# Output projections of a two-layer decoder trunk: all sums and low parts on VectorE, the first projection's sums made in layer A's heads, two plain tiles at the head of pass two

## The chip, the core and the metric

The kernel runs on one core of a Trainium2 chip. The metric is the device time of one execution in microseconds (us), as the median of several runs.

## The reference

One inference step of a trunk with two layers. The input is 1024 prompt tokens and 8 sample tokens, T = 1032 columns of 1024 features. Layer A is an HGRN2 mixer with 8 heads, layer B a chunked gMLP. Each ends in an output projection from 2048 to 1024 features, a residual add, and a gated per-layer embedding:

```python
# layer A
return (o * jax.nn.silu(z)) @ w_out, S          # z, o: (B, L, 2048), w_out: (2048, 1024)
# layer B
y = (u * s * jax.nn.silu(z)) @ w_out
# trunk, in each layer
h = h + y
gate = jax.nn.sigmoid(rmsnorm(h, norm_ple[i]) @ w_ple_gate[i])
h = h + gate * (p[i] @ w_ple_proj[i])
```

The change touches the two products with `w_out` and what lies just around them.

## The kernel before, in words

**Columns.** The 1032 tokens stand in the free dimension, in three column groups c = 0, 1, 2 of 384, 384 and 264. An output tile m (0 to 7) is 128 output features. The product's input, 2048 features deep, was stored to DRAM by the mixer as `ozd[c]`, 16 blocks of 128 features.

**Precision.** Every fp32 product is three products of rounded operands (`mm3`, lines 222 to 224): high x high, high x low, low x high. An operand's high part is a ScalarE (ACT) copy, its low part a subtraction (`split`, lines 217 and 218; in lists of loads lines 370 and 373; for weights 149 and 150). The low part's buffer is called `xml` or `bl`, the high part's `xmh` or `bh`.

**Units.** For columns c = 0 and 1 and two output tiles m, m+1 together, `unit` computes a 2 x 2 block product with seven block products instead of eight (twelve matmuls each): it needs sums of weight blocks (s1 to s4, made by GpSimd, the POOL engine, lines 191 to 198) and sums of data blocks (t1 to t4, made by `mix_rows`, lines 963 to 966). ACT copies the first product to `u2` (line 914). VectorE (DVE) adds further products to it at lines 918, 930, 937, 944 and 950. Line 937 gives `c` (the tile `c22`) from the bank `ps_d`. The unit's seventh product is added up in that same bank, so TensorE (PE) must wait for line 937 when it has done the sixth. Column group 2 is done plainly (24 matmuls of 264 columns a tile). A plain tile has 24 matmuls for each of the three groups.

**Projection.** `out_phase` runs twice: for layer A from about 760 to 960 us, for layer B from about 1624 to 1820. It goes over the depth in two passes f of 1024 features. Pass f=0: plain tiles 0 and 1, then units m = 2, 4, 6. Pass f=1: units m = 0, 2, 4, then plain tiles 6 and 7. Beside the plain tiles of pass one, `mix_first` makes the first half's sums and splits. During units m = 2 and 4, `mix_second` makes those of the second half and stores them to DRAM. During unit m = 6 the second half's blocks and sums replace the first half's: `jobs` loads them through seven buffers (three `zr`, four `raw`) in list order, each waiting for its high and low part. The low parts alternate between VectorE and GpSimd. `add` (line 1036) adds a result to the residual rows `h`: from PSUM on VectorE, from SBUF in pass one on GpSimd. In pass two `accum_sq` squares the new rows on ACT (line 257, into one of four `tmp` buffers), and GpSimd adds the squares up (line 258).

**Order.** TensorE's order is the order of the code. The other engines' streams, SP's queue of transfers among them, are put in order by a scheduler by readiness and priorities. Each stream then runs in that order. An instruction that waits holds up all behind it on its engine.

Of the kernel before, what the change touches and what calls it, by code (L numbers as in the profile page):

```python
# [17 lines left out]
P = 128  # L18
# [63 lines left out]
def trunk_kernel(ctx, tc, xT, st, pT, nrm, wina, lbl, gna, wouta, winb, lng, lnb, lngr, lnbr,  # L82
# [161 lines left out]
    def accum_sq(sp, ssq, src, first, last, w, eng=G):  # L244
# [3 lines left out]
        sq = sp.tile([P, 384], F32, name="sql", bufs=1) if last else sp.tile([P, 384], F32, name="tmp", bufs=4)  # L248
# [154 lines left out]
    def p_in_act(l, stage, load=True):  # L403
# [7 lines left out]
        return ([fh[:, :, OFF[c]:OFF[c] + W[c]] for c in CH], [fl[:, :, OFF[c]:OFF[c] + W[c]] for c in CH])  # L411

# [548 lines left out]
    def mix_rows(b11, b12, b21, b22, eng=V):  # L961

        V.tensor_tensor(b11, b12, b11, ALU.subtract)
        eng.tensor_tensor(b12, b22, b12, ALU.subtract)
        V.tensor_tensor(b22, b22, b11, ALU.subtract)
        V.tensor_tensor(b21, b21, b22, ALU.subtract)

    tdr = {}

    def out_phase(key, b, ssq, first, done, pre, begin):  # L970
# [3 lines left out]
        with ExitStack() as s:  # L974
# [14 lines left out]
            def quarters(k, rows):  # L989

                for (c, o), t in zip(((0, 0), (1, 0), (0, 4), (1, 4)), rows):
                    nc.sync.dma_start(t, ozd[c][:, k + o, :])


            rows = [[hr[c][2 * j + i] for i in range(2) for c in (0, 1)] for j in range(4)]
            if pre:
                rows[0] = [raw() for _ in range(4)]
            begin(up, raw, rows, quarters, load_h)

            def mix_first():  # L1000
                for j in range(4):
                    mix_rows(*rows[j], G)
                    for n, t in (("t2", rows[j][3]), ("t1", rows[j][0]), ("t3", rows[j][1])):
                        split(b[n][0][:, j, :], b[n][1][:, j, :], t, G if n == "t3" else V)
                    if not j and not pre:
# [37 lines left out]
            tk.spawn(mix_first(), 1)  # L1043
# [6 lines left out]
            for c in CH:  # L1050
                add(1, c, plain(pp.tile([P, 384], F32, name="ps_o1", tag=("pA", "po", "pt")[c], bufs=1), wt, c), False)
                if c == 1:
                    while any(p[2].__name__ == "mix_first" for p in tk.procs):
# [8 lines left out]
            if not tdr:  # L1062
                for n in ("t1", "t2", "t3", "t4"):
                    tdr[n] = dram.tile([P, 4, 384], F32, name="d" + n)

            def mix_second():
                for j in range(4):
# [5 lines left out]
                    for n, x in zip(("t1", "t3", "t4", "t2"), t):  # L1073
                        nc.sync.dma_start(tdr[n][:, j, :], x)
# [4 lines left out]
            def quarter(n, to=None):  # L1079
                src = {"b11": ozd[0][:, 8:12], "b21": ozd[0][:, 12:16], "b12": ozd[1][:, 8:12],  # L1080
                       "b22": ozd[1][:, 12:16]}.get(n)
                src = tdr[n] if src is None else src
                return [(src[:, k, :], b[to or n][0][:, k, :], b[to or n][1][:, k, :], 384) for k in range(4)]

            def jobs():
# [4 lines left out]
                turns = itertools.cycle([zr] * ZR + [lambda w: raw()[:, :w]] * 4)  # L1090
# [485 lines left out]
```

## Time and profile before

| | us |
|---|---|
| runs, median (lowest to highest, 3 runs) | 1933.72 (1931.68 to 1934.5) |
| profiled execution | 1930.22 |
| its span | 1928.5 |
| PE busy | 1870.2 |
| DVE busy | 1329.4 |
| ACT busy | 865.7 |
| POOL busy | 586.9 |

The profiled execution lies 3.5 us under the median. The mean granted TensorE clock was 0.986 of full speed. Busy time is shown for each engine. In a row of a timeline stand the start, the duration, engine, line, operation, output <- inputs, and in brackets the idle time before it with what ended it. A row of a window has its bounds, its length, the busy time and the count of instructions by engine, the granted clock, the share of the DMA engines and GB/s.

### The profile page before, as it was taken

The page shows a single profiled execution, that of the slowest core. Times are in us where ns is not written, and L with a number is a line of the kernel's source. Part 1 is how long each engine was busy: PE and PEld are TensorE (multiplying, and loading weights), DVE is VectorE, ACT ScalarE, POOL GpSimd, SP SyncE. Part 2 cuts the span into 40 slices and gives each one's busy share as a digit, 9 for nine tenths or more (in the row PEclk, how much of TensorE's full clock was granted, in tenths as well). Part 3 has the DMA queues.
Part 4 walks back from the last instruction along what each step waited for, and adds up shares of the span by engine and source line. Part 5 has one row for each costly group of instructions (what it writes and reads, how often), then busy time and mean ns, then how long its engine had stood idle before and what let it go on. Part 6 is the DMA issues. An engine that isn't in the chain of part 4 may idle for free.

```text
span 1928.5 us, 34355 instructions
## 1 busy us (share of the span) xinstructions
PE 1870.2 (97%) x13106; PEld 1840.3 (95%) x13106; DVE 1329.4 (69%) x2841; ACT 865.7 (45%) x1855; POOL 586.9 (30%) x563
## 2 busy tenths in 40 slices
PE   9999999999999999889999999999999999989997
PEld 8999999999999998889999999999999999889997
DVE  5967776776767676877564755577777777875655
ACT  6463544444454546344343544433434435343342
POOL 4110000001000100466432433345445442565421
PEclk8999999999999999999999999999999999999998
DMA  6232322222231326773233343323333237762223
GB/s 212 74 118 65 115 67 102 78 80 89 80 107 50 110 93 186 252 228 105 81 119 123 123 141 91 99 80 102 130 109 105 100 116 227 237 212 73 70 89 110
DMA packets 145109, 228.98 MB, mean 119 GB/s; under 512 B 13936, under 2 KB 120112, under 8 KB 143920
## 3 DMA queue, kind: packets, MB, share of 16 engines
q1 hardware_dynamic: 144944, 226.78, 36.1%
q8 instruction: 103, 1.69, 0.4%
q14 instruction: 62, 0.51, 0.1%
HBM read 167.62 MB, written 59.11 MB: 118 GB/s over the span
## 4 chain that ended last, share of the span: by engine, by line
PE 77%; DVE 8%; DMA 7%; issue 3%; POOL 2%; ACT 2%; SPq 1%; DVEq 0%; ACTq 0%; POOLq 0%
PE ps_proj L222 19%; PE ps_proj L224 19%; PE ps_proj L223 19%; PE ps_d L222 2%; PE ps_d L224 2%; PE ps_d L223 2%; DMA raw<-ozd 1%; PE psp L1376 1%; PE pC L679 1%; DVE wlo L150 1%; PE pt_o L725 1%; PE pss L272 1%; DMA dt<-raw 1%; PE p L645 1%; PE ps_o L222 1%
## 5 line engine op out<-in xcount | busy, mean ns | idle before, releaser
L222 PE MATMUL ps_proj<-bh,whi 128*128 128x384 f32 (+1 forms) x2448 | 784.7, 321 | 4.1 <-ACT pple_t L341 1.6
L224 PE MATMUL ps_proj<-bh,wlo 128*128 128x384 f32 (+1 forms) x2448 | 768.8, 314 | 3.1 <-DVE wlo L150 2.8
L223 PE MATMUL ps_proj<-bl,whi 128*128 128x384 f32 (+1 forms) x2448 | 767.4, 313 | 2.2 <-POOL bl L218 2.2
L222 PEld LDWEIGHTS ps_proj<-bh,whi 128*128 128x128 f32 x2448 | 464.2, 190 | 6.4 <-ACT pple_t L341 1.7
L223 PEld LDWEIGHTS ps_proj<-bl,whi 128*128 128x128 f32 x2448 | 464.4, 190 | 2.9 <-POOL bl L218 2.9
L224 PEld LDWEIGHTS ps_proj<-bh,wlo 128*128 128x128 f32 x2448 | 462.7, 189 | 4.5 <-DVE wlo L150 4.5
L150 DVE TENSOR_TENSOR wlo<-wstg,whi 128x1024 fp32r<-128x1024 f32 x148 | 193.7, 1308 | 107.1 <-ACT whi L149 106.0
L149 ACT CAST whi<-wstg 128x1024 fp32r<-128x1024 f32 x148 | 155.0, 1048 | 152.0 <-PE ps_proj L223 140.7
L149 ACT CAST shi<-ssum 128x512 fp32r<-128x512 f32 x136 | 84.0, 620 | 164.7 <-PE ps_proj L223 78.0
L150 DVE TENSOR_TENSOR slo<-ssum,shi 128x512 fp32r<-128x512 f32 x136 | 110.0, 810 | 23.3 <-ACT shi L149 23.0
L258 POOL TENSOR_TENSOR ssq<-ssq,tmp 128x384 f32<-128x384 f32 (+1 forms) x72 | 75.5, 1051 | 155.7 <-ACT tmp L257 146.8
L218 POOL TENSOR_TENSOR ql<-q,qh 128x384 fp32r<-128x384 f32 (+1 forms) x24 | 22.3, 928 | 254.5 <-ACT qh L217 254.5
L222 PE MATMUL ps_proj<-xmh,shi 128*128 128x384 f32 x248 | 84.3, 340 | 2.4 <-ACT xmh L217 2.1
L223 PE MATMUL ps_proj<-xml,shi 128*128 128x384 f32 x248 | 83.4, 336 | 2.3 <-DVE xml L218 2.3
L191 POOL TENSOR_TENSOR ssum<-wstg 128x512 f32<-128x512 f32 x34 | 50.3, 1480 | 111.4 <-DMA wstg<-in_winb 75.2
L231 POOL TENSOR_TENSOR rsq<-ss_e,mhalf 128x3 f32<-128x3 f32 (+2 forms) x32 | 24.1, 752 | 195.4 <-DVE ss_e L719 195.4
L224 PE MATMUL ps_proj<-xmh,slo 128*128 128x384 f32 x248 | 83.2, 336 | 0.0
L682 DVE TENSOR_TENSOR q<-q,t 128x192 f32<-128x192 f32 (+1 forms) x144 | 47.2, 329 | 44.5 <-PE pC L679 38.2
L257 ACT ACTIVATE tmp<-h 128x384 f32<-128x384 f32 (+1 forms) x72 | 35.3, 491 | 91.9 <-DVE h L1131 49.2
L193 POOL TENSOR_TENSOR ssum<-ssum,wstg 128x512 f32<-128x512 f32 x34 | 45.6, 1341 | 95.3 <-DVE slo L150 95.3
L1385 POOL TENSOR_TENSOR s<-s,u 128x384 f32<-128x384 f32 (+1 forms) x48 | 53.1, 1106 | 68.9 <-DVE s L1379 68.3
L1130 DVE TENSOR_TENSOR tmp<-tmp,pj 128x384 f32<-128x384 f32 (+1 forms) x48 | 25.0, 521 | 56.6 <-ACT tmp L1129 47.1
(330 smaller groups left out, 4062.2 us busy)
## 6 DMA issues: line engine op xcount, KB each, us to landing
wstg<-in_wina SPq DMA_DIRECT2D x48, 512.0 KB, 3.6
wstg<-in_winb SPq DMA_DIRECT2D x48, 512.0 KB, 4.4
raw<-ozd SPq DMA_DIRECT2D x44, 192.0 KB, 3.5
pj<-ppd SPq DMA_DIRECT2D x16, 516.0 KB, 4.8
S<-in_st SPq DMA_DIRECT2D x16, 512.0 KB, 5.3
vb<-vd SPq DMA_DIRECT2D x16, 512.0 KB, 4.6
out_so_s<-S SPq DMA_DIRECT2D x16, 512.0 KB, 3.4
wstg<-in_wouta SPq DMA_DIRECT2D x16, 512.0 KB, 4.5
```

What stands on the lines that cost most here:

```text
L149: A.copy(hi, src)
L150: V.tensor_tensor(lo, src, hi.bitcast(F32), ALU.subtract)
L191: G.tensor_tensor(t, a21, a22, ALU.add)
L193: G.tensor_tensor(t, t, a11, ALU.subtract)
L222: PE.matmul(ps, wh, xh, start=first, stop=False, skip_group_check=more)
L223: PE.matmul(ps, wh, xl, start=False, stop=False, skip_group_check=more)
L224: PE.matmul(ps, wl, xh, start=False, stop=last, skip_group_check=more)
L257: A.activation(sq[:, :w], src, AF.Square)
L258: eng.tensor_tensor(ssq, ssq, sq[:, :w], ALU.add)
L682: V.tensor_tensor(ql[:, :, 1, :], ql[:, :, 1, :], t2[:, :, 0:1].broadcast_to([P, n, lv]), ALU.mult)
L1130: V.tensor_tensor(gt[:, :w], gt[:, :w], pj[:, OFF[c]:OFF[c] + w], ALU.mult)
L1385: G.tensor_tensor(s[:, :w], s[:, :w], us[mm, c][:, :w], ALU.mult)
```

## The change

1. `mix_rows`, the low parts of the projections and the adds to `h` all run on VectorE. In each projection four subtractions and four low parts of the first sums, nine adds, and the low parts that alternated in the list of loads leave GpSimd. It keeps the weight sums and the sums of squares.
2. For the first projection, the sums of the first half are made by `mix_early` beside the heads of layer A: 16 loads, 16 subtractions and 16 stores of 192 KB. The projection then loads the sums in place of the blocks.
3. Pass two begins with plain tiles 0 and 1 in place of unit m = 0.
4. The second half's plain blocks are loaded ahead of its sums, into other buffers than before, and the loads go on between the plain tiles.
5. The squares of a projection's tiles go through one buffer, `sql`.

The core of the diff:

```diff
@@ out_order: the order of the weights, and so of the output tiles
-                [("O" + l, m, 1) for m in range(0, KT - 2, 2)] + [("o" + l, m, 1) for m in range(KT - 2, KT)])
+                [("o" + l, m, 1) for m in range(2)] + [("O" + l, m, 1) for m in range(2, KT - 2, 2)] +
+                [("o" + l, m, 1) for m in range(KT - 2, KT)])
@@ accum_sq
-    def accum_sq(sp, ssq, src, first, last, w, eng=G):
+    def accum_sq(sp, ssq, src, first, last, w, eng=G, own=False):
...
-        sq = sp.tile([P, 384], F32, name="sql", bufs=1) if last else sp.tile([P, 384], F32, name="tmp", bufs=4)
+        sq = sp.tile([P, 384], F32, name="sql", bufs=1) if last or own else sp.tile([P, 384], F32, name="tmp", bufs=4)
@@ mix_rows and quarters move up, out of out_phase
-    def mix_rows(b11, b12, b21, b22, eng=V):
+    def mix_rows(b11, b12, b21, b22):
...
-        eng.tensor_tensor(b12, b22, b12, ALU.subtract)
+        V.tensor_tensor(b12, b22, b12, ALU.subtract)
...
+    TS = ("t1", "t2", "t3", "t4")
+    tdr = [{n: dram.tile([P, 4, 384], F32, name=f"d{i}{n}") for n in TS} for i in range(3)]
+
+    def store_sums(d, j, rows):
+        for n, x in zip(("t1", "t3", "t4", "t2"), rows):
+            nc.sync.dma_start(d[n][:, j, :], x)
@@ in the heads of layer A
+    def mix_early():
+
+        for j in range(4):
+            t = [wa.tile([P, 2, 384], F32, name="zstg", bufs=2) for _ in range(2)]
+            t = [x[:, i, :] for x in t for i in range(2)]
+            quarters(j, t)
+            yield 8
+            mix_rows(*t)
+            store_sums(tdr[0], j, t)
+            yield 6
...
     for h in range(NH):
+        if h == 5:
+            tk.spawn(mix_early(), 4)
@@ out_phase: first sums
-            def mix_first():
+            def sums_first():
                 for j in range(4):
-                    mix_rows(*rows[j], G)
-                    for n, t in (("t2", rows[j][3]), ("t1", rows[j][0]), ("t3", rows[j][1])):
-                        split(b[n][0][:, j, :], b[n][1][:, j, :], t, G if n == "t3" else V)
+                    if not ahead:
+                        mix_rows(*rows[j])
+                    for n in ("t2", "t1", "t3"):
+                        split(b[n][0][:, j, :], b[n][1][:, j, :], rows[j][at[n]])
@@ out_phase: adds
-                eng = V if end or src.space == PSUM else G
                 with tc.high_priority(offset=PRI if end and m >= KT - 2 else 0):
-                    eng.tensor_tensor(hr[c][m], hr[c][m], src[:, :W[c]], ALU.add)
+                    V.tensor_tensor(hr[c][m], hr[c][m], src[:, :W[c]], ALU.add)
                 if end:
-                    accum_sq(sp, ssq[c], hr[c][m], c not in seen, m == KT - 1, W[c])
+                    accum_sq(sp, ssq[c], hr[c][m], c not in seen, m == KT - 1, W[c], own=True)
@@ out_phase: the exchange of halves, and pass two
-                todo = quarter("b11") + quarter("t2") + quarter("b21")
-                todo += [(ozd[2][:, 8 + k, :], b["c2"][0][:, k, :], b["c2"][1][:, k, :], W[2]) for k in range(8)]
-                todo += quarter("t1") + quarter("t3") + quarter("b22") + quarter("t4")
-                return load_list(todo, lambda w: next(turns)(w), ZR + 4, False, (V, G), True)
-                        then = {2: 4, 3: 4, 4: 4, 5: 8, 6: 4, 7: 4}
-                    elif (f, m) == (1, 0):
-                        then = {3: 4, 4: 4}
+                o = dict(b)
+                for n, to in (("b11", "b11"), ("b21", "t2"), ("b12", "b21"), ("b22", "t1"),
+                              ("t2", "t3"), ("t1", "b22"), ("t3", "t4"), ("t4", "b21")):
+                    b[n] = o[to]
+                todo = quarter("b11") + quarter("b21") + quarter("b12") + quarter("b22")
+                todo += [(ozd[2][:, 8 + k, :], b["c2"][0][:, k, :], b["c2"][1][:, k, :], W[2]) for k in range(8)]
+                todo += quarter("t2") + quarter("t1") + quarter("t3") + quarter("t4")
+                gen[0] = load_list(todo, lambda w: next(turns)(w), ZR + 4, False, (V,), True)
...
+            units(0, range(2, KT, 2), {2: (rows_of(2), {4: 1}), 4: (rows_of(4), {2: 1, 4: 1, 7: 1}),
+                                       KT - 2: (exchange, {2: 4, 3: 4, 4: 4, 6: 4, 7: 4})})
+            for m in range(2):
+                wt = take(key, m, 1)
+                for c in CH:
+                    ps = plain(bank(), wt, c)
+                    if (m, c) != (1, 2):
+                        steps(gen[0], 4)()
+                    add(m, c, ps, True)
+            units(1, range(2, KT - 2, 2), {KT - 4: (last_exchange, {4: 4})})
@@ begin of the first projection
-            quarters(j, rows[j])
+            for n, t in zip(("t1", "t3", "t4", "t2"), rows[j]):
+                nc.sync.dma_start(t, tdr[0][n][:, j, :])
```
How this moves instructions is shown at three places. The first is VectorE in unit m = 6 of the first projection, the last rows up to the `c` result, before:

```order
1555 L1036 TENSOR_TENSOR h_6_10170<-h_6_10170,ps_proj 128x384
1556 L150 TENSOR_TENSOR wlo<-wstg,whi 128x1024
1557 L373 TENSOR_TENSOR xml_10147<-zr,xmh_10146 128x384
1558 L373 TENSOR_TENSOR bl_123<-zr,bh_120 128x384
1559 L1036 TENSOR_TENSOR h_7_10187<-h_7_10187,ps_proj 128x264
1560 L373 TENSOR_TENSOR bl_123<-raw,bh_120 128x384
1561 L373 TENSOR_TENSOR bl_125<-raw,bh_122 128x264
1562 L930 TENSOR_TENSOR u_11063<-ps_proj,u_10963 128x384
1563 L150 TENSOR_TENSOR slo<-ssum,shi 128x512
1564 L373 TENSOR_TENSOR bl_125<-zr,bh_122 128x264
1565 L373 TENSOR_TENSOR bl_125<-raw,bh_122 128x264
1566 L937 TENSOR_TENSOR c_11094<-ps_d,u_11063 128x384
```
and after:

```order
1568 L374 TENSOR_TENSOR xml_10215<-raw,xmh_10214 128x384
1569 L1057 TENSOR_TENSOR h_6_10238<-h_6_10238,ps_proj 128x384
1570 L151 TENSOR_TENSOR wlo<-wstg,whi 128x1024
1571 L374 TENSOR_TENSOR xml_10215<-raw,xmh_10214 128x384 x2
1572 L374 TENSOR_TENSOR xml_10215<-zr,xmh_10214 128x384
1573 L1057 TENSOR_TENSOR h_7_10255<-h_7_10255,ps_proj 128x264
1574 L374 TENSOR_TENSOR bl_135<-zr,bh_132 128x384 x2
1575 L374 TENSOR_TENSOR bl_135<-raw,bh_132 128x384
1576 L963 TENSOR_TENSOR u_11083<-ps_proj,u_10983 128x384
1577 L374 TENSOR_TENSOR bl_135<-raw,bh_132 128x384
1578 L374 TENSOR_TENSOR xml_10213<-raw,xmh_10212 128x384
1579 L970 TENSOR_TENSOR c_11114<-ps_d,u_11083 128x384
```
Line 373 is now 374, 930 is 963, 937 is 970, 1036 is 1057. Before, every other low part is here (the rest is on GpSimd), and three of group 2 (264 columns) and a weight sum's low part (`slo`) stand just ahead of `c`. Now all are here, in list order, group 2 comes behind `c`, and no `slo` stands ahead of it. Between the last sum (line 419) and the first of these rows stand four more low parts and the result of line 951 (918 before).

The second place is VectorE at the start of the first projection, where sums (963, 965, 966) and low parts (218) alternate with adds, before:

```order
1478 L963 TENSOR_TENSOR h_2_10166<-h_2_10174,h_2_10166 128x384
1479 L1036 TENSOR_TENSOR h_0_10180<-h_0_10180,ps_o 128x264
1480 L150 TENSOR_TENSOR wlo<-wstg,whi 128x1024
1481 L965 TENSOR_TENSOR h_3_10175<-h_3_10175,h_2_10166 128x384
1482 L218 TENSOR_TENSOR xml_10145<-h_2_10166,xmh_10144 128x384
1483 L966 TENSOR_TENSOR h_3_10167<-h_3_10167,h_3_10175 128x384
1484 L218 TENSOR_TENSOR xml_10147<-h_3_10175,xmh_10146 128x384
1485 L150 TENSOR_TENSOR slo<-ssum,shi 128x512 x2
1486 L963 TENSOR_TENSOR h_4_10168<-h_4_10176,h_4_10168 128x384
```
and after (low parts are line 219, adds 1057):

```order
1487 L219 TENSOR_TENSOR xml_10213<-raw,xmh_10212 128x384
1488 L219 TENSOR_TENSOR xml_10217<-raw,xmh_10216 128x384
1489 L151 TENSOR_TENSOR slo<-ssum,shi 128x512
1490 L1057 TENSOR_TENSOR h_0_10232<-h_0_10232,ps_o 128x384
1491 L1057 TENSOR_TENSOR h_0_10240<-h_0_10240,ps_o 128x384
1492 L219 TENSOR_TENSOR xml_10215<-raw,xmh_10214 128x384
1493 L1057 TENSOR_TENSOR h_0_10248<-h_0_10248,ps_o 128x264
1494 L151 TENSOR_TENSOR slo<-ssum,shi 128x512
1495 L151 TENSOR_TENSOR wlo<-wstg,whi 128x1024
1496 L219 TENSOR_TENSOR xml_10215<-h_3_10243,xmh_10214 128x384
1497 L219 TENSOR_TENSOR xml_10213<-h_2_10234,xmh_10212 128x384
```
The sums are gone from this place; the low parts of t1, t2 and t3 stand together.

The third is SP's queue in a head of layer A, with weight loads (`wstg`), stores of the head's result (`ozd`) and of the state (`out_so_p`), before:

```order
74 L163 DMA wstg<-in_wina 128x1024
75 L781 DMA ozd_73<-oz 128x768
76 L757 DMA out_so_p<-S 128x256
77 L163 DMA wstg<-in_wina 128x1024
78 L781 DMA ozd_74<-oz 128x768
79 L781 DMA ozd_75<-oz 128x2x264
80 L163 DMA wstg<-in_wina 128x1024 x3
```
and after, where line 424 loads the blocks and line 431 stores the sums:

```order
80 L801 DMA ozd_74<-oz 128x768
81 L424 DMA zstg<-ozd_74 128x384
82 L801 DMA ozd_75<-oz 128x2x264
83 L431 DMA d0t_119<-zstg 128x384
84 L431 DMA d0t_118<-zstg 128x384
85 L164 DMA wstg<-in_wina 128x1024
86 L431 DMA d0t_120<-zstg 128x384
87 L424 DMA zstg<-ozd_73 128x384
88 L424 DMA zstg<-ozd_74 128x384
89 L424 DMA zstg<-ozd_73 128x384
90 L424 DMA zstg<-ozd_74 128x384
91 L431 DMA d0t_117<-zstg 128x384
```
Loads and stores of the sums now stand between the weight loads; a store waits there for VectorE's subtraction.

More of the change, by code (lines that the diff above doesn't have):

```diff
@@ L1052, in out_phase @@
                 if c == 1:
-                    while any(p[2].__name__ == "mix_first" for p in tk.procs):
+                    while any(p[2].__name__ == "sums_first" for p in tk.procs):
                         tk.tick()
@@ L1059, in out_phase @@
                         load_h(m)
-            if not tdr:
-                for n in ("t1", "t2", "t3", "t4"):
-                    tdr[n] = dram.tile([P, 4, 384], F32, name="d" + n)
+            d = tdr[1 if first else 2]
             def mix_second():
@@ L1117, in out_phase, with rows_of, go @@
-            b["b12"] = b["t1"]
+                    ex, hooks = then.get(m, (None, {}))
+                    bb = dict(b)
+                    if ex:
+                        ex()
+                    unit(wt, bb, up, lambda i, c, src: add(m + i, c, src, f == 1),
+                         early=int(f == 0 and m in (2, KT - 2)),
+                         then={i: (lambda n=n: [next(gen[0], None) for _ in range(n)]) for i, n in hooks.items()})
+            gen = [mixer]
+            def rows_of(m):
+                def go():
+                    for i in (2, 3):
+                        load_h(m + i)
+                return go
@@ new lines, in exchange @@
+            def exchange():
+                assert next(mixer, None) is None
+                o = dict(b)
[5 more added lines that the diff above has]
+                todo += quarter("t2") + quarter("t1") + quarter("t3") + quarter("t4")
+                turns = itertools.cycle([zr] * ZR + [lambda w: raw()[:, :w]] * 4)
+                gen[0] = load_list(todo, lambda w: next(turns)(w), ZR + 4, False, (V,), True)
+                steps(gen[0], ZR + 4)()
@@ L1445, in trunk_kernel, with begin @@
     ssq3 = new_ssq()
-    def begin(up, raw, rows, quarters, load_h):
+    def begin(up, raw, rows, load_h):
         place = itertools.cycle([(up, n, 2, 384) for n in ("u2", "u2", "u4", "u4", "c22", "c22")] + [(ws[0], "ssum", 2, 512)] * 2)
```

60 lines of the change are left out of this document (24 added, 36 removed).

## The prediction, made before the changed kernel was run

> **What bounds the kernel now.** I read the page first, then stretches of the span, then TensorE's waits in the two output projections, then the engines it waits for.
>
> ```profile
> PE 1870.2 (97%) x13106; PEld 1840.3 (95%) x13106; DVE 1329.4 (69%) x2841; ACT 865.7 (45%) x1855; POOL 586.9 (30%) x563
> ```
>
> TensorE bounds the whole. What is left to win lies where it idles or runs at a lower granted clock. The stretches (busy us of each engine, then the clock) show one head of layer A, then both output projections:
>
> ```profile
> 180.00:270.00 90.00, 89.57 (x713) 87.32 (x712) 63.25 (x186) 42.87 (x111) 7.16 (x13) 1.00 0.28 89
> 760.00:960.00 200.00, 186.15 (x1165) 183.79 (x1164) 139.89 (x196) 80.61 (x151) 104.54 (x84) 0.97 0.53 172
> 1640.00:1800.00 160.00, 144.72 (x894) 142.76 (x893) 114.49 (x154) 62.05 (x113) 92.48 (x73) 0.96 0.53 170
> ```
>
> A head leaves 0.43 us idle. The first projection leaves 13.85, the second 15.28. TensorE's waits in windows around each (740 to 990, then 1600 to 1860):
>
> ```profile
> PE ps_d L222 <- DVE c L937: 8.8, 3, 5.2
> PE ps_proj L223 <- DVE xml L218: 2.3, 1, 2.3
> PE ps_proj L222 <- ACT xmh L217: 2.1, 1, 2.1
> ...
> PE ps_d L222 <- DVE c L937: 12.5, 4, 6.8
> ```
>
> The largest item is `c`, VectorE's copy out of the unit's fifth product, on whose bank the seventh product goes on. In time order (the bracket is the idle time before the matmul):
>
> ```profile
> 799.60 0.44 PE L222 MATMUL ps_proj<-xmh,shi 128*128 128x384 f32 x1 [2.06 <-ACT xmh L217]
> 802.34 0.69 PE L223 MATMUL ps_proj<-xml,shi 128*128 128x384 f32 x1 [2.30 <-DVE xml L218]
> 835.40 0.44 PE L222 MATMUL ps_d<-bh,whi 128*128 128x384 f32 x1 [1.40 <-DVE c L937]
> 864.19 0.69 PE L222 MATMUL ps_d<-bh,whi 128*128 128x384 f32 x1 [5.24 <-DVE c L937]
> 886.90 0.41 PE L222 MATMUL ps_d<-bh,whi 128*128 128x384 f32 x1 [2.16 <-DVE c L937]
> ...
> 1723.54 0.69 PE L222 MATMUL ps_d<-xmh,whi 128*128 128x384 f32 x1 [6.75 <-DVE c L937]
> 1746.11 0.41 PE L222 MATMUL ps_d<-xmh,whi 128*128 128x384 f32 x1 [3.20 <-DVE c L937]
> ```
>
> Behind the long stalls the granted clock (third number from the end) is down:
>
> ```profile
> 800.00:808.00 8.00, 5.06 (x22) 4.70 (x22) 8.00 (x11) 3.05 (x5) 3.42 (x3) 0.79 0.27 78
> 864.00:872.00 8.00, 7.81 (x29) 7.81 (x30) 8.00 (x10) 5.44 (x11) 8.00 (x7) 0.60 0.64 197
> 888.00:896.00 8.00, 8.00 (x48) 8.00 (x47) 5.24 (x9) 3.64 (x7) 4.63 (x4) 0.82 0.20 68
> 1648.00:1656.00 8.00, 5.74 (x35) 5.34 (x34) 7.85 (x14) 2.27 (x6) 3.11 (x3) 0.79 0.19 62
> 1720.00:1728.00 8.00, 4.46 (x16) 4.46 (x17) 8.00 (x10) 6.22 (x14) 7.60 (x8) 0.57 0.76 212
> 1744.00:1752.00 8.00, 5.89 (x31) 5.92 (x32) 6.61 (x11) 2.38 (x5) 2.83 (x3) 0.79 0.22 79
> ```
>
> Eight us times one minus the clock: 1.7, 3.2, 1.4; 1.7, 3.4, 1.7. The first projection so loses 6.7 (5.0 idle, 1.7 clock) at its start, 1.4 near 835, 8.4 at the exchange of halves, 3.6 near 887. The second loses 7.0 at its start and in small stalls (5.33 of the 15.28, and 1.7), 10.2 at the exchange, 4.9 near 1746. Together 42.2 us, all that the change can win.
>
> The Trainium skill ("TensorE: Matmul & The Clock Gate", "Part 1: The HAM clock gate") has the clock fall only after an idle window of about 3.4 us. By it the stalls of 2 us here would cost no clock, and the gain below would be some 4.8 us smaller. The rows disagree: after stalls of 2.06 and 2.30 the clock was 0.79. I go by the rows.
>
> **Why VectorE is late.** It works alongside GpSimd:
>
> ```profile
> 795.85 0.55 DVE L966 TENSOR_TENSOR h<-h,h 128x384 f32<-128x384 f32 x1
> 799.39 1.36 DVE L966 TENSOR_TENSOR h<-h,h 128x384 f32<-128x384 f32 x1
> 846.18 0.56 DVE L966 TENSOR_TENSOR raw<-raw 128x384 f32<-128x384 f32 x1
> 851.63 0.56 DVE L373 TENSOR_TENSOR bl<-raw,bh 128x384 fp32r<-128x384 f32 x1 [2.12 <-ACT bh L370]
> 854.07 1.23 DVE L150 TENSOR_TENSOR wlo<-wstg,whi 128x1024 fp32r<-128x1024 f32 x1
> 856.51 1.36 DVE L373 TENSOR_TENSOR bl<-zr,bh 128x384 fp32r<-128x384 f32 x1
> 863.59 0.54 DVE L937 TENSOR_TENSOR c<-ps_d,u 128x384 f32<-128x384 f32 x1
> ...
> 799.03 1.30 POOL L218 TENSOR_TENSOR xml<-h,xmh 128x384 fp32r<-128x384 f32 x1 [0.62 <-ACT xmh L217]
> 856.13 1.33 POOL L373 TENSOR_TENSOR bl<-zr,bh 128x384 fp32r<-128x384 f32 x1
> ```
>
> The same VectorE operation takes 0.55 us when GpSimd is idle and 1.36 beside a GpSimd operation. `c`, with one operand in PSUM, takes 0.54 in the thick of it. So each operation given to GpSimd costs VectorE about 0.81 us, more than the 0.55 it would take there. From 846 to `c` the low parts of L373 take so much of VectorE, then of GpSimd (count in brackets):
>
> ```profile
> 846.00:863.60 17.60, 9.08 (x9) 10.30 (x10) 1.00 0.80 240
> ```
>
> **The change part by part.** The sum is made against the profiled execution (1930.2 us) and shifted to the median, 3.5 higher.
>
> *Exchange in unit m=6.* `c` must be there when the sixth product ends, 5.24 us before 864.19: about 858.7, 12.5 us after the last sum at 846.2. Before, VectorE needed 17.4. In the new order 13 low parts, two results, two adds and one weight low part stand between: 13 x 0.55 + 2 x 0.55 + 2 x 0.42 to 0.54 + 1.2 = 10.5, plus waits for loads (2.1 before 851.63 now). That is 12.5: just in time. Bounds for what stays: 0, and 5.2 plus clock. I leave 2.0 of 8.4 and, for the longer stall of the second projection, 2.5 of 10.2: -6.4 and -7.7.
>
> *Two plain tiles open pass two.* They read first what is loaded first, and give 22 us for the other low parts while no `c` waits behind them. The stalls near 887 and 1746 came from VectorE's backlog; I leave 0.5 each: -3.1 and -4.4. Price: a unit is 7 x 12 + 2 x 24 matmuls, two plain tiles 4 x 24 + 2 x 24, so 12 more of 384 columns, at 0.17 between starts:
>
> ```profile
> 858.44 0.33 PE L223 MATMUL ps_proj<-bl,shi 128*128 128x384 f32 x1
> 858.62 0.34 PE L224 MATMUL ps_proj<-bh,slo 128*128 128x384 f32 x1
> ```
>
> That is +2.1 in each projection. The four weight sums and their splits that fall away lie beside TensorE and count nothing.
>
> *First projection's sums in the heads.* 16 subtractions leave its start, where VectorE was busy 8.00 of 8 us. 12 of them were VectorE's, so the last low part of t2 comes about 12 x 0.55 = 6.6 us and the contention earlier, against stalls of 5.0. The loads are as many as before. I leave 1.5 of 6.7: -5.2. In the heads they cost 16 x 0.55 = 8.8 us of VectorE and 32 transfers on SP's queue. The cover is VectorE's 27 idle us in 90. If it fails, TensorE waits for `oz`, as it does a little already:
>
> ```profile
> PE pt_o L725 <- DVE oz L774: 2.6, 6, 0.4
> ...
> raw<-ozd SPq DMA_DIRECT2D x44, 192.0 KB, 3.5
> ```
>
> Bounds: 0, and 8.8 plus three rounds of store and load not covered (2 x 3.5 each), 30. A head has room for that, so near the lower end: +1.5.
>
> *Second projection's start.* Its sums stay there, now all on VectorE: eight operations more (4.4 us), against contention of about 0.15 us on each of 21. Nothing won, nothing lost; with the small stalls -0.5. Near 835 also -0.5.
>
> *Adds on VectorE.* 9 per projection at 0.55, 5 us in 60: hidden, as the lone `c` waits there are small.
>
> *One buffer for the squares.* ACT must wait for GpSimd's add before the next square:
>
> ```profile
> L258 POOL TENSOR_TENSOR ssq<-ssq,tmp 128x384 f32<-128x384 f32 (+1 forms) x72 | 75.5, 1051 | 155.7 <-ACT tmp L257 146.8
> ```
>
> The last tiles end some 0.5 us later: +1.0 for both. Below nothing it can't be.
>
> Sum: first -6.4 -3.1 -5.2 -0.5 +2.1 = -13.1; second -7.7 -4.4 -0.5 +2.1 = -10.5; heads and squares +2.5. That is -21.1: 1909 beside the profiled execution, 1912.6 beside the median, said as 1912.
>
> **The rivals.**
>
> *Loads set the pace of the exchange.* Seven buffers, 3.5 us a load plus the turn through ACT, at up to 0.7 us a low part, and traffic packed closer than the 240 GB/s of the row above. Then `c` comes as late as half of now: 4.2 and 5.1 lost instead of 2.0 and 2.5, and part of the stalls after it, some 9 us back: 1921. For it speaks the 2.12 us wait at 851.63; against it that only 13 low parts, not 19, precede `c`.
>
> *Every stall goes.* -42.2 + 4.2 for the tiles + 2.5: 1898. Against it: the second projection's start does not get lighter.
>
> *Slower: VectorE saturates.* If 1.36 us were VectorE's own time, 13 x 1.36 + 3.5 = 21 us would stand before `c`, 4 more than now in each projection; the second's start would take 7 us more, the heads and squares 2.5, the tiles 4.2, against -5.2 at the first start: +16, 1950. With d the time of a low part, the result is nought near d = 0.55 + 0.81 x 21/37 = 1.0 us. GpSimd keeps weight sums and square adds, so d won't be 0.55 everywhere; but the 0.56 row stands in the very stretch. The Trainium skill ("Perfetto Trace Analysis", "Optimizing Scalar/DVE Operations") advises moving work off a saturated VectorE, which speaks for this rival, but adds that between these two engines it might not help since they share a port.
>
> *The squares block ACT.* In pass two ACT's copy of a unit's first product stands behind a square, which waits for GpSimd, which may sit in a weight sum. A wait of one sum and one add, 2.5 us, in four units, partly covered by the second product's 2.1 us: 2 to 10 us, 1916 to 1922. It joins the first rival's time.
>
> *No change.* The stalls move to the next late operand: 1930 to 1936.
>
> **How the numbers follow.** Forecast 1912 (its own range 1905 to 1917) 0.55; loads or squares 0.22; every stall gone 0.10; no change 0.07; saturation 0.06. A measurement of this kernel tells about 0.2% (4 us) from no change. Faster 0.87, same 0.07, slower 0.06. The range takes in the second and third case and stops at the border of no change: 1898 to 1929.
>
> **What would show it.** After the change: GpSimd's low parts and adds are gone and VectorE's low parts at the exchange take 0.55 to 0.7; `c` waits total under 5 us per projection; the stalls at the first start are gone, those at the second's start remain; the heads still idle about half a us; a clock of 1.00 in nearly all slices. I am wrong if VectorE's low parts stay over 1 us, if ACT's high parts wait on loads, or if a head idles over 2 us.

## The result: 1912.06 us against 1934.11, a ratio of 0.989

| | median us (lowest to highest) | profiled execution's span | mean clock |
|---|---|---|---|
| before | 1934.11 (1931.68 to 1935.4) | 1928.5 | 0.986 |
| changed | 1912.06 (1911.88 to 1913.87) | 1912.2 | 0.991 |

The ratio is 0.989 with a 95% interval of 0.9872 to 0.9907: 1.1% faster. The spans of the two profiled executions differ by 16.3 us only, the medians by 22: before's profiled execution (1930.22) lay under all its timed ones, the changed kernel's (1913.87) was the slowest of its four. A later comparison in more runs (the last of the experiments) gave 0.9917, which is the 16 to 17 us of the traces.

The page of the changed kernel: TensorE's share goes from 97 to 98%, GpSimd (POOL) is busy 101 us less, and VectorE (DVE), which does more operations, is busy 9 us less.

```profile
PE 1866.9 (98%) x13130; PEld 1837.2 (96%) x13130; DVE 1320.7 (69%) x2905; ACT 862.9 (45%) x1853; POOL 486.1 (25%) x481
```

A head that makes sums, and both projections (the second now begins some 10 us earlier):

```profile
270.00:360.00 90.00, 89.57 (x711) 87.32 (x710) 66.60 (x192) 43.43 (x113) 8.02 (x13) 1.00 0.38 122
760.00:960.00 200.00, 192.69 (x1221) 190.99 (x1220) 131.34 (x221) 79.70 (x152) 57.09 (x47) 0.97 0.55 179
1630.00:1790.00 160.00, 151.36 (x960) 148.88 (x958) 114.76 (x189) 62.39 (x115) 47.36 (x36) 1.00 0.55 181
```

The head still leaves 0.43 us idle, though VectorE is busy 66.6 us in it and 122 GB/s move. The projections leave 7.3 and 8.6 us where they left 13.85 and 15.28. TensorE's stalls that remain (the bracket is the idle time before the matmul):

```profile
810.74 0.69 PE L223 MATMUL ps_d<-bh,whi 128*128 128x384 f32 x1 [3.35 <-DVE c L970]
831.41 0.45 PE L223 MATMUL ps_d<-bh,whi 128*128 128x384 f32 x1 [0.23 <-DVE c L970]
857.62 0.69 PE L223 MATMUL ps_d<-bh,whi 128*128 128x384 f32 x1 [2.66 <-DVE c L970]
888.71 0.44 PE L223 MATMUL ps_proj<-xmh,whi 128*128 128x384 f32 x1 [0.59 <-ACT u L947]
...
1643.73 0.39 PE L225 MATMUL ps_proj<-bh,wlo 128*128 128x264 f32 x1 [1.68 <-DVE wlo L151]
1709.23 0.44 PE L223 MATMUL ps_d<-xmh,whi 128*128 128x384 f32 x1 [2.77 <-DVE c L970]
1737.31 0.44 PE L223 MATMUL ps_proj<-xmh,shi 128*128 128x384 f32 x1 [1.17 <-DVE h L1057]
```

The long waits at the exchange (5.24, 6.75) are 2.66 and 2.77 now. The stalls at the first start are gone. One stands where none of its size stood: 3.35 us for `c` of unit m=2. VectorE in the exchange, from the last sum (L419) up to `c` with some rows left out, then ACT's high parts that the last of these low parts waits for:

```profile
843.11 0.55 DVE L419 TENSOR_TENSOR raw<-raw 128x384 f32<-128x384 f32 x1
...
848.06 0.56 DVE L374 TENSOR_TENSOR bl<-raw,bh 128x384 fp32r<-128x384 f32 x1 [2.52 <-ACT bh L371]
...
853.35 0.55 DVE L374 TENSOR_TENSOR bl<-raw,bh 128x384 fp32r<-128x384 f32 x1
...
854.28 0.55 DVE L374 TENSOR_TENSOR bl<-raw,bh 128x384 fp32r<-128x384 f32 x1
856.54 0.56 DVE L374 TENSOR_TENSOR xml<-raw,xmh 128x384 fp32r<-128x384 f32 x1 [1.71 <-ACT xmh L371]
857.02 0.55 DVE L970 TENSOR_TENSOR c<-ps_d,u 128x384 f32<-128x384 f32 x1
...
856.00 1.06 ACT L371 CAST xmh<-raw 128x384 fp32r<-128x384 f32 x2 [2.80 <-DMA raw<-ozd]
```

Every low part there takes 0.55 us, and GpSimd has no row in this stretch. What keeps `c` is two of the 13 low parts, the fourth and the thirteenth, whose high parts wait for their loads: 2.52 and 1.71 us. The new stall in unit m=2 has its cause in weights that come late. First SP's issue of the weights for m=4, then GpSimd, then VectorE:

```profile
793.30 0.91 SPq L188 DMA_DIRECT2D wstg<-in_wouta  x2
...
801.28 1.28 POOL L192 TENSOR_TENSOR ssum<-wstg 128x512 f32<-128x512 f32 x1 [19.41 <-DMA wstg<-in_wouta]
...
803.25 1.11 DVE L151 TENSOR_TENSOR slo<-ssum,shi 128x512 fp32r<-128x512 f32 x1 [6.42 <-ACT shi L150]
```

The weights issued from 793.3 to 794.2 are there at 801.2. VectorE stands 6.42 us at a weight sum's low part, and behind it wait the adds, a weight low part, two sums and `c`, which came at 810.14.

### The profile page after: what moved, and what is told of

It is laid out like the page before. It is cut to its first block, busy times and chain, and to the rows that moved or that the text cites. A ratio compares the mean times of both kernels' runs of the same rounds, so it can differ in the third digit from the quotient of the medians.

```text
span 1912.2 us, 34401 instructions
## 1 busy us (share of the span) xinstructions
PE 1866.9 (98%) x13130; PEld 1837.2 (96%) x13130; DVE 1320.7 (69%) x2905; ACT 862.9 (45%) x1853; POOL 486.1 (25%) x481
## 3 DMA queue, kind: packets, MB, share of 16 engines
q8 instruction: 103, 1.69, 0.4%
## 4 chain that ended last, share of the span: by engine, by line
PE 77%; DVE 9%; DMA 7%; issue 2%; ACT 2%; POOL 2%; SPq 1%; DVEq 0%; ACTq 0%; POOLq 0%
PE ps_proj L223 19%; PE ps_proj L225 19%; PE ps_proj L224 19%; DMA raw<-ozd 2%; PE ps_d L223 2%; PE ps_d L225 2%; PE ps_d L224 2%; DVE wlo L151 1%; PE psp L1414 1%; PE pC L699 1%; PE pt_o L745 1%; PE pss L273 1%; PE p L665 1%; PE ps_o L223 1%; PE ps_o L224 1%
## 5 line engine op out<-in xcount | busy, mean ns | idle before, releaser
L223 PE MATMUL ps_proj<-bh,whi 128*128 128x384 f32 (+1 forms) x2392 | 765.2, 320 | 3.3 <-ACT u L947 1.7
L225 PE MATMUL ps_proj<-bh,wlo 128*128 128x384 f32 (+1 forms) x2392 | 749.6, 313 | 4.3 <-DVE wlo L151 4.1
L224 PE MATMUL ps_proj<-bl,whi 128*128 128x384 f32 (+1 forms) x2392 | 748.5, 313 | 0.9 <-DVE bl L219 0.9
L223 PEld LDWEIGHTS ps_proj<-bh,whi 128*128 128x128 f32 x2392 | 451.4, 189 | 5.2 <-ACT u L947 2.7
L225 PEld LDWEIGHTS ps_proj<-bh,wlo 128*128 128x128 f32 x2392 | 450.3, 188 | 5.8 <-DVE wlo L151 5.8
L224 PEld LDWEIGHTS ps_proj<-bl,whi 128*128 128x128 f32 x2392 | 451.7, 189 | 2.1 <-DVE bl L219 1.6
L151 DVE TENSOR_TENSOR slo<-ssum,shi 128x512 fp32r<-128x512 f32 x128 | 103.9, 812 | 24.0 <-ACT shi L150 23.7
L223 PE MATMUL ps_o<-bh,whi 128*128 128x384 f32 (+1 forms) x232 | 73.2, 315 | 0.0
L224 PE MATMUL ps_o<-bl,whi 128*128 128x384 f32 (+1 forms) x232 | 72.7, 313 | 0.0
L225 PE MATMUL ps_o<-bh,wlo 128*128 128x384 f32 (+1 forms) x232 | 72.6, 313 | 0.0
```

The source lines that it names most:

```text
L151: V.tensor_tensor(lo, src, hi.bitcast(F32), ALU.subtract)
L223: PE.matmul(ps, wh, xh, start=first, stop=False, skip_group_check=more)
L224: PE.matmul(ps, wh, xl, start=False, stop=False, skip_group_check=more)
L225: PE.matmul(ps, wl, xh, start=False, stop=last, skip_group_check=more)
```

## The experiments

"Loss" in the table is worked out from windows of 8 us between 760 and 912 and between 1616 and 1768 us: TensorE's idle time plus eight times one minus the clock, both projections together, in the profiled execution. It stands for one execution: the two of the changed kernel differ by 1.8 us. The windows are fixed in time, and before's row holds 1.1 us of a wait at 1620 that falls ahead of them in the faster kernels. The ratio is to runs of the kernel before that were made beside it.

| run | ratio (95% interval) | loss us |
|---|---|---|
| before | 1 | 43.9 |
| changed kernel | 0.989 (0.9872 to 0.9907) | 20.6 |
| changed kernel again | 0.9917 (0.9901 to 0.9933) | 18.8 |
| v_alone | 0.9911 (0.9896 to 0.9925) | 21.2 |
| low_only | 0.9963 (0.9951 to 0.9975) | 33.7 |
| gp_back | 1.0028 (1.0017 to 1.0038) | 39.9 |
| sums_late | 0.9908 (0.9893 to 0.9923) | 20.0 |
| unit_opens | 0.9891 (0.9875 to 0.9906) | 20.1 |
| four_squares | 0.9892 (0.9873 to 0.9912) | 15.8 |
| unit_squares | 0.9909 (0.9893 to 0.9924) | 20.3 |
| gp_reads | 0.9923 (0.9904 to 0.9941) | 23.4 |
| gp_writes | 0.9901 (0.9887 to 0.9914) | 17.2 |
| c_first | 0.9907 (0.9891 to 0.9923) | 20.3 |
| rows_later | 0.9949 (0.9936 to 0.9963) | 27.6 |

**v_alone: the kernel before, VectorE does all.**

```diff
-                    mix_rows(*rows[j], G)
+                    mix_rows(*rows[j])
-                        split(b[n][0][:, j, :], b[n][1][:, j, :], t, G if n == "t3" else V)
+                        split(b[n][0][:, j, :], b[n][1][:, j, :], t)
-                eng = V if end or src.space == PSUM else G
+                eng = V
-                return load_list(todo, lambda w: next(turns)(w), ZR + 4, False, (V, G), True)
+                return load_list(todo, lambda w: next(turns)(w), ZR + 4, False, (V,), True)
-                        gen = load_list(quarter("b12", "t1"), zr, ZR, False, (V, G))
+                        gen = load_list(quarter("b12", "t1"), zr, ZR, False, (V,))
```

> The kernel before with one thing changed: all sums, low parts and adds of the projections on VectorE, in the old order of loads and tiles. Theory (VectorE's long low parts come from GpSimd beside it): its low parts at the exchange take 0.55 to 0.7 us, the two long waits for c (5.24 and 6.75 us) fall to about 3, those near 887 and 1746 to under 1.5, the starts stay; 1920 us, 14 under the kernel before. Rival (the 1.36 us are VectorE's own): the waits grow by 4 us each, 1945.

Measured: 1912.63 us, 0.9911. This one part brings about the whole gain. It was more than I expected (1920), since the starts got lighter too: TensorE's stalls at the first go from 2.06, 2.30 and 0.65 to 1.55, 0.42 and 1.69, and the first projection's exchange looks like this, TensorE's stalls and then VectorE's last sum and `c`:

```profile
855.18 0.44 PE L222 MATMUL ps_d<-bh,whi 128*128 128x384 f32 x1 [1.28 <-DVE c L937]
863.79 0.44 PE L222 MATMUL ps_proj<-bh,whi 128*128 128x384 f32 x1 [2.07 <-ACT u L914]
877.23 0.44 PE L223 MATMUL ps_d<-bl,whi 128*128 128x384 f32 x1 [0.84 <-DVE bl L373]
...
841.96 0.55 DVE L966 TENSOR_TENSOR raw<-raw 128x384 f32<-128x384 f32 x1
854.58 0.55 DVE L937 TENSOR_TENSOR c<-ps_d,u 128x384 f32<-128x384 f32 x1
```

`c` starts 12.6 us after the last sum, where it started 17.4 us after it before. VectorE makes 13 low parts in between instead of nine, so a shorter queue ahead of `c` is not the reason: the nine took 9.1 us (two of them of 264 columns), the 13 take 6.7 (one of them of 264). (1.1 us of the 4.8 are shorter waits for loads.) The page of v_alone says what GpSimd's help had been worth over the whole kernel:

```profile
PE 1862.0 (98%) x13106; PEld 1830.7 (96%) x13106; DVE 1328.0 (70%) x2915; ACT 867.3 (45%) x1855; POOL 505.5 (26%) x489
```

VectorE does the 74 operations that GpSimd did, and is busy 1328.0 us instead of 1329.4. So on the average an operation given to GpSimd had held VectorE up about as long as it takes on VectorE, some 0.55 us (an estimate from these two rows). GpSimd's help was worth nothing to VectorE's busy time.

**gp_back: the changed kernel, GpSimd's share put back.** `load_list` gets (V, G) again, the t3 low parts, one subtraction in four and the adds from SBUF in pass one go to GpSimd; all else of the change stays.

> The changed kernel with GpSimd's share put back: every other low part of the loads, the first sums' t3 low parts, one subtraction in four at the second projection's start, the adds of pass one. The sums in the heads, the plain tiles at the head of pass two, the loads' order and the one square buffer stay. Theory (moving the work to VectorE is the whole gain): long low parts come back, waits for c of 4 us and more at the exchanges with their clock; 1924 to 1932 us. Rival (the other parts carry half of it): 1918 to 1921.

Measured: 1934.44 us, 1.0028: slower than the kernel before by 0.17 to 0.38%, and above the theory's 1932. Without VectorE's part the rest of the change is a loss. Waits for `c` of 3.50, 2.50, 1.56 and 3.91 us are back, and a wait of a new kind, at the start of pass two's first unit, in both projections:

```profile
892.43 0.69 PE L223 MATMUL ps_proj<-xmh,whi 128*128 128x384 f32 x1 [4.39 <-ACT u L947]
...
889.62 0.99 POOL L374 TENSOR_TENSOR bl<-raw,bh 128x384 fp32r<-128x384 f32 x1
890.57 0.98 POOL L259 TENSOR_TENSOR ssq<-ssq,sql 128x384 f32<-128x384 f32 x1
...
891.59 0.42 ACT L258 ACTIVATE sql<-h 128x264 f32<-128x264 f32 x1 [4.40 <-POOL ssq L259]
891.92 0.46 ACT L947 COPY u<-ps_proj 128x384 f32<-128x384 f32 x1
```

This is the prediction's rival on the squares: with one buffer, ACT waits 4.40 us for a GpSimd add that stands behind two weight sums and a low part, and its copy `u` stands behind the square. So 8.4 of the 22 us that gp_back loses to the changed kernel are waits that only the one buffer makes possible.

**low_only: the kernel before, only the low parts of the loads on VectorE** (the last two edits of v_alone).

> The kernel before with only the low parts of the loaded blocks all on VectorE; the first sums, their t3 low parts and the adds of pass one keep GpSimd. Theory (the exchange, and the waits for c after it, are where GpSimd beside VectorE costs most; the starts are the smaller part): the long waits fall as in the kernel where VectorE does all, the 5.0 us at the first start stay; 1916 to 1920 us. Rival (the adds beside the low parts collide as much): 1924 or more.

Measured: 1921.62 us, 0.9963, between theory and rival. Of v_alone's 0.9% the loads' low parts are 0.4. The stalls at the first start stay at 2.05 and 2.30 us, and those at the exchange fall to 2.35 and 1.57. So the first sums with their low parts and the adds are some half of it (0.5, with an uncertainty of 0.2). The prediction had put the adds and the second projection's sums at nothing.

**gp_reads and gp_writes: idle GpSimd work beside the low parts.** In the changed kernel, behind every second one of the first 16 low parts of each exchange:

```diff
+                if behind and i % 2 and i < lag + 16:
+                    dm = gpt[0]()                                  # the buffer sql
+                    G.tensor_tensor(dm, zh, zh, ALU.add)           # gp_reads
+                    G.tensor_copy(dm[:, :1], zh[:, :1])            # gp_writes, with the next two
+                    G.memset(dm[:, :384], 0.0)
+                    G.memset(dm[:, :384], 0.0)
```

> The changed kernel with eight idle additions on GpSimd in each exchange, from the high parts in SBUF; nothing waits for their results, and VectorE's order is the same, row by row. Theory (a GpSimd operation that reads SBUF holds up VectorE's operations with two SBUF operands): low parts beside them go from 0.55 to 1.0 to 1.4 us, c comes 2 to 4 us later than in the changed kernel (waits of 2.7 and 2.8 us become about 5 and 6); 1917 to 1920 us. Rival (the low parts were long because VectorE had too much, not because of GpSimd): 0.55 stays, 1912 us.

> The same with GpSimd only writing: a copy of one column to tie it to the high part, then two fills of the same buffer, at the same eight places. Theory (reading is what collides): VectorE's low parts stay at 0.55 us and the waits for c as in the changed kernel, 1912 us. Rival (any GpSimd work in SBUF collides): low parts over 0.8 us and 1917 us or more.

Measured: gp_reads 1915.56 us, 0.9923; gp_writes 1909.97 us, 0.9901. The waits for `c` at the exchanges were 4.18 and 4.72 us with reads (forecast: 5 and 6), 2.77 and 2.81 with fills. Without either they were 2.66 and 2.77, and 3.83 and 2.64 in the second trace of the changed kernel, so that only the 4.72 stands clear of it. VectorE's rows for the same four instructions, with GpSimd reading (the first of them two low parts), and GpSimd's row beside:

```profile
849.05 1.65 DVE L376 TENSOR_TENSOR xml<-raw,xmh 128x384 fp32r<-128x384 f32 x2
850.62 1.18 DVE L376 TENSOR_TENSOR xml<-zr,xmh 128x384 fp32r<-128x384 f32 x1
851.72 0.42 DVE L1064 TENSOR_TENSOR h<-h,ps_proj 128x264 f32<-128x264 f32 x1
852.06 1.30 DVE L376 TENSOR_TENSOR bl<-zr,bh 128x384 fp32r<-128x384 f32 x2
...
850.36 2.12 POOL L379 TENSOR_TENSOR sql<-bh 128x384 f32<-128x384 f32 x2
```

and with GpSimd filling:

```profile
845.24 1.02 DVE L376 TENSOR_TENSOR xml<-raw,xmh 128x384 fp32r<-128x384 f32 x2
846.17 0.55 DVE L376 TENSOR_TENSOR xml<-zr,xmh 128x384 fp32r<-128x384 f32 x1
846.64 0.42 DVE L1066 TENSOR_TENSOR h<-h,ps_proj 128x264 f32<-128x264 f32 x1
846.98 1.02 DVE L376 TENSOR_TENSOR bl<-zr,bh 128x384 fp32r<-128x384 f32 x2
...
846.37 0.42 POOL L381 MEMSET sql<- 128x384 f32 x1
```

VectorE's order is the same in both. The operation grows from 0.55 to 1.18 us beside a reading GpSimd operation and stays at 0.55 beside a fill; the add from PSUM takes 0.42 in both. This settles that GpSimd operations that read SBUF make the low parts long, and that VectorE was not just too full. The Trainium skill ("SBUF — State Buffer", "Who interferes with whom") states it so: a VectorE instruction with two SBUF inputs contends with a GpSimd instruction that reads SBUF, not with one that only writes. The rows agree, with 1.18 us against 0.55. By time, the two intervals overlap a little, and 1915.56 us lies under the theory's 1917 to 1920; the durations carry the verdict. How the gain divides between VectorE's shorter rows and GpSimd being the slower worker was not tried: its own low parts of 384 columns took 1.0 to 1.65 us at the exchange of the kernel before, and each holds its staging buffer so long.

**sums_late: the first projection's sums at its start again.**

```diff
-        if h == 5:
-            tk.spawn(mix_early(), 4)
...
-                    if not ahead:
-                        mix_rows(*rows[j])
+                    mix_rows(*rows[j])
```

> The changed kernel, with the first projection's sums made at its start again (on VectorE) and not in the heads. Theory (what the heads save at the start, the earlier rush of loads gives back, since the weights of unit m=4 then come late and VectorE waits 6.4 us behind their sum): the start loses 4 us, the 3.35 us wait for c at 810 and its clock loss (3.4) go; 1909 to 1913 us, no difference from 1912. Rival (the sums in the heads are worth their forecast 5 us): 1917.

Measured: 1912.46 us, 0.9908, not to be told from the changed kernel. At the start 1.62 and 0.42 us come back, and the 3.35 us in unit m=2 are gone, as the theory said. But its exchange waited 4.12 us, with a clock of 0.57 behind it. So the sums in the heads have no measurable worth. That what they save comes back at the exchange is not shown: the unedited changed kernel, too, has waited 3.83 us there, and its wait in m=2 varies (below).

**rows_later: residual rows of tiles 4 to 7 one unit later.** `load_h` for them is issued behind the first stores of the second half's sums.

> The changed kernel with the residual rows of tiles 4 to 7 loaded one unit later, behind the first stores of the second half's sums. Theory (the weights for m=4 take 8 us to land because these and other loads share the transfer engines): weights land about 3 us earlier, the wait of 3.35 us for c at 810 falls under 1 and its clock loss (3.4) goes; 1906 to 1908 us. Rival (the weights are late because their buffer frees late, or the four block loads ahead of them fill the engines): the wait stays above 2, 1911 to 1913.

Measured: 1919.54 us, 0.9949, slower than the changed kernel. The wait in m=2 fell to 1.56, but not as the theory said: the weights came 2.9 us earlier (798.4), but they were also issued 2.6 us earlier (790.7 against 793.3), and they still took some 7 us to land. In place of the wait in m=2, m=4 waits 4.48 us (4.88 in the second projection), since the second half's blocks were late and VectorE stood at a sum ahead of `c`:

```profile
830.12 0.69 PE L223 MATMUL ps_d<-bh,whi 128*128 128x384 f32 x1 [4.48 <-DVE c L970]
...
827.15 0.56 DVE L416 TENSOR_TENSOR raw<-raw 128x384 f32<-128x384 f32 x1 [4.35 <-DMA raw<-ozd]
```

The wait in m=2 also varies by itself: eight executions with the same code up to there (the changed kernel's two, four_squares, c_first, both gp runs, unit_opens, unit_squares) had 1.18 to 3.35 us, with weights that came at 797.6 to 802.6. So the 1.56 of this run says less than it seems.

**c_first: the thirteenth low part behind `c`.**

```diff
+                with tc.issue_after(rest["c22"].ins) if behind and i >= lag + 12 else ExitStack():
+                    engines[...].tensor_tensor(zl, stg[i - lag], zh.bitcast(F32), ALU.subtract)
```

> The changed kernel with the thirteenth and later low parts of the exchange put behind c on VectorE. Theory (c waits 1.7 and 2.1 us behind one low part whose load is not there): the waits of 2.66 and 2.77 us before the seventh product of m=6 fall under 0.7, the clock loss of 1.7 goes; 1905 to 1908 us. Rival (the time comes back at once as a wait for the b22 blocks in the first plain tile): 1911.

Measured: 1911.01 us, 0.9907; the rival was right. The waits at the exchanges fell to 1.48 and 0.48 us, and between the plain tiles of the first projection these came (1.06, 1.03 and 1.75 in the second):

```profile
883.00 0.41 PE L223 MATMUL ps_proj<-bh,whi 128*128 128x384 f32 x1 [1.65 <-DVE h L1058]
886.35 0.44 PE L223 MATMUL ps_proj<-xmh,shi 128*128 128x384 f32 x1 [1.02 <-DVE h L1058]
890.45 0.44 PE L223 MATMUL ps_proj<-xmh,whi 128*128 128x384 f32 x1 [1.75 <-ACT u L948]
```

**unit_opens: pass two opens with unit m=0, loads in the old order, all on VectorE. four_squares: four square buffers. unit_squares: both.**

> The changed kernel with pass two in the old order: unit m=0 first, blocks and sums loaded in the old order, low parts all on VectorE. Theory (the plain tiles take TensorE's waits for c after the exchange away, for 2.1 us each): TensorE has 4.2 us less work, waits for c near 880 and 1735 of 1 to 3 us each come back with their clock, and group 2's low parts stand ahead of c; 1916 us. Rival (with GpSimd silent, VectorE has no backlog any more, and the tiles only cost): 1908.

> The changed kernel with four buffers for the squares again. Theory (ACT's wait for the one buffer is hidden, the tail costs 0.5 us a projection): 1911 us, not to be told from 1912; waits of TensorE for ACT's copy u (0.59, 0.76, 0.50) stay. Rival (the one buffer holds up ACT's copies in pass two): 1908 or less, and the waits for u in pass two go.

> The changed kernel with pass two opened by unit m=0 in the old order and four buffers for the squares: VectorE's part and the sums in the heads are all that is left of the change. Theory (the plain tiles and the one buffer bring nothing, the tiles cost 2.1 us of TensorE each): 1908 to 1910 us, the fastest by 2 to 3 us. Rival (the plain tiles pay for themselves): 1912.

Measured: 1909.71, 1909.79 and 1910.33 us; 0.9891, 0.9892 and 0.9909. All three agree with the changed kernel's two ratios. In unit_opens, TensorE has 4.2 us less to do, and waits for low parts whose sums come late from DRAM:

```profile
862.11 0.44 PE L223 MATMUL ps_proj<-bh,whi 128*128 128x384 f32 x1 [2.81 <-ACT u L947]
875.65 0.44 PE L224 MATMUL ps_d<-bl,whi 128*128 128x384 f32 x1 [0.84 <-DVE bl L374]
...
ACT xmh L371 <- DMA raw<-d1t: 6.2, 3, 3.8
```

Behind the exchange unit_opens idles 4.8 and 3.6 us (first, second projection), where the changed kernel idles 0.6 and 1.7; at the exchange it waits 1.24 and 0.53 where the changed kernel waits 2.66 and 2.77. So the tiles shorten the stalls behind the exchange, as forecast, and lengthen those before it. The loss is about the same (20.1 against 20.6 and 18.8), and the work of TensorE is 4.2 us more. The times lie 2 to 3 us lower without the tiles, which these intervals can't tell from nothing. In four_squares the waits for `u` after the plain tiles (0.59, 0.50) are gone, but the changed kernel's second trace had none and 0.38 us, and the time, between the theory's 1911 and the rival's 1908, does not show them. No version was measurably faster than the changed kernel.

**changed_again: the changed kernel, unedited.**

> The changed kernel itself, unedited, in more runs beside the kernel before. The two traces explain 16 to 17 us, the medians of the first comparison differ by 22. If the traces tell the size, the ratio is 0.991 to 0.992 (16 to 17 us); if the first comparison does, 0.989 (21 to 22 us). The wait for c in unit m=2 varies between 1.4 and 3.4 us.

Measured: 1912.57 us (1907.79 to 1915.54) against 1929.41 (1924.84 to 1932.56), a ratio of 0.9917 with 0.9901 to 0.9933: 16.8 us, so the traces tell the size. The kernel before ran at 1934 in the first comparison and at 1929 to 1932 in the later ones, and that made up the rest. In this trace `c` waits 1.18 us in m=2 (under the expected 1.4), and 3.83 and 2.64 at the exchanges.

## Why the prediction was right, and where its steps were off

The forecast was 1912 (1898 to 1929), the median 1912.06. The mechanism was right in its main part: v_alone and gp_back show that the work taken off GpSimd is the whole gain, and the gp runs that GpSimd's reads make VectorE's low parts long. That the number fits to a microsecond is chance: the sum was -21.1, the spans differ by 16.3 and the larger comparison by 16.8. It fell on the median because the median that the sum started from, 1933.72, lay 2 to 5 us above the kernel's later ones. Of the 42.2 us of loss 21.6 went, and 4.2 of work came in with the plain tiles; that makes 17.4, of which the spans show 16.3.

| term | forecast to stay | stayed |
|---|---|---|
| first start (6.7) | 1.5 | 0 |
| unit m=2 of the first projection | none | 3.35 + 3.4 clock |
| near 835 (1.4) | 0.9 | 0.23 |
| exchange, first (8.4) | 2.0 | 2.66 + 1.7 clock |
| near 887 (3.6) | 0.5 | 0.59 |
| second start and small stalls (7.0) | 6.5 | 4.2 |
| exchange, second (10.2) | 2.5 | 2.77 |
| near 1746 (4.9) | 0.5 | 1.67 |
| sum | 14.4 | 20.6 |

- *The price of 0.81 us.* "Each operation given to GpSimd costs VectorE about 0.81 us, more than the 0.55" was read from one of the longest rows. v_alone puts the average at some 0.55: even, not a loss. The gain does not hang on it, but it was the reason given.
- *First start.* Right that it goes; wrong that this is a gain. The step failed at "the loads are as many as before": TensorE reached unit m=2 some 5 us sooner, and the weights for m=4 did not (800.3 before, 801.3 now). This was in no term. In sums_late the weights are there at 793.7, and the wait in m=2 is gone.
- *Exchange.* The count of 13 low parts at 0.55 us held. The mis-sized term is the waits for loads, put at 2.1 us: they are 2.52 and 1.71 here, 4.2 together, and `c` starts 13.9 us after the last sum, where 12.5 were allowed. Two loads set the stall now, where GpSimd's reads did.
- *Second start.* "Nothing won" was wrong: with GpSimd's share gone, 4.2 us stay of 7.0, and no clock loss in this trace. In 45 us there (1620 to 1665 before, 1612 to 1657 now) VectorE does nine operations more (61 against 52) in about the same busy time (33.85 us against 33.54), so the contention cost more than the 0.15 us an operation that I took from a mean.
- *Two plain tiles.* The price of +2.1 each is right in count (24 matmuls more on the page). Of the credit of -3.1 and -4.4 the stalls behind the exchange show something, but they came back ahead of it: unit_opens loses no more in all without the tiles.
- *Adds on VectorE, called hidden.* low_only against v_alone gives the adds and the first sums with their low parts together half of the gain. Which of them was not tried.
- *Heads, +1.5.* Nothing: 0.43 us idle as before.
- *Squares, +1.0.* Up to twice 0.5 us, not at the tail but before the first unit of pass two. The rival's mechanism is real, and in gp_back it costs 4.4 and 4.0 us.
- *Rivals and signs.* One sign of being wrong came true: ACT's high parts wait on loads, 2.80 us in the row above (the sum itself had allowed for 2.1). With `c` waits of 6.24 us in the first projection, over the 5 that were said, the first rival holds in its mechanism, though not in its time of 1921. Loads do set the pace now: c_first took one wait away and got it back as another, and rows_later got back more than it took. Saturation of VectorE is refuted by the 0.55 us rows and by v_alone.

Not settled: how much of the remaining 19 to 21 us of loss belongs to the loads alone. A version with fewer bytes to load, or more staging buffers, was not tried.

## What to carry to other kernels

Before giving VectorE's work to GpSimd, compare a VectorE row of two SBUF operands beside a GpSimd operation with one alone, and then VectorE's whole busy time with and without the help: here single rows grew by up to 0.81 us, and 74 operations on GpSimd saved VectorE nothing. Change that first and measure it alone: the first of the change's five parts did the work of all five. When several waits on different engines go back to loads, removing one of them can move it to the next, and the sum to look at is all idle time and clock loss of the stage.

## What the runs showed of the hardware

- A GpSimd fill or one-column copy in SBUF leaves VectorE's subtraction of two SBUF operands at 0.55 us, a GpSimd addition beside it makes it 1.18 (gp_writes, gp_reads).
- The clock does not follow the length of the stall alone. In the changed kernel 2.66 us (up to 857.62) cost 1.7 us of clock in the first projection and 2.77 us (up to 1709.23) cost none in the second; in its second trace 2.64 us at that place cost 1.7. The granted clock is the third number from the end:

```profile
856.00:864.00 8.00, 6.38 (x28) 6.38 (x29) 7.32 (x16) 6.15 (x14) 0.00 (x0) 0.79 0.71 205
...
1704.00:1712.00 8.00, 5.23 (x31) 4.91 (x30) 5.91 (x14) 3.97 (x10) 0.00 (x0) 1.00 0.72 234
1712.00:1720.00 8.00, 8.00 (x49) 8.00 (x47) 6.67 (x15) 4.23 (x9) 0.20 (x1) 1.00 0.76 236
```

The Trainium skill ("TensorE: Matmul & The Clock Gate", "Part 1: The HAM clock gate") says that the window is free-running, so that the point of change varies by where it lies. That would fit these rows, but no run here shows the window. The idle window of about 3.4 us that it puts ahead of the lower clock does not fit: 2.66 us were followed by a clock of 0.79, and the measurement decides.
